# Alternating the pairs of an MLP's first product, using one raw weight buffer less per pair, and tying the row splits of its second product to its sums

## The chip, the cores and the metric

The kernel runs on one core of a Trainium2 chip. The metric is device time in microseconds (us) of one launch, median of three runs. In the profile PE is the matrix engine (TensorE), PEld its weight loads, DVE VectorE, ACT ScalarE, POOL GpSimd, and SP the engine that here only issues DMAs. "Lnnn" is a line of the kernel. A row such as "SPq" or "ACTq" is that engine's issuing side.

## The reference

One decoder layer for 1024 prompt tokens and 64 sample tokens (1088 in all), 1024 features. After a mixing part (an input projection, an RWKV-7 branch, a pooling branch, a merge), which the change does not touch, comes the channel mixer:

```
sh, sc, gt = ada_mod(c, lp["w_ada_mlp"], lp["b_ada_mlp"])
h = rms_norm(x, lp["norm_mlp"]) * (1 + sc) + sh
x = x + gt * (jnp.square(jax.nn.relu(h @ lp["w_ff1"])) @ lp["w_ff2"])
...
y = rms_norm(x, W["norm_final"])
```

`w_ff1` is 1024 x 4096 and `w_ff2` 4096 x 1024, all in fp32.

## The kernel before, in words

**A product.** Features lie on the 128 partitions, tokens along the free dimension. An fp32 matmul is made of three faster ones: each operand is split into a rounded part "hi" and a remainder "lo" (ACT copies hi, DVE or POOL subtracts to get lo), and hi·hi, hi·lo and lo·hi are added in PSUM. For weights `halves` does this (L186 to L195): a raw weight tile of 128 x 512 goes through ACT at L193 (`whi`) and DVE or POOL at L194 (`wlo`).

**The first MLP product (`ff1`, L1629)** works on 16 pairs `j`. A pair is two blocks of 128 hidden features; with the two halves of the input features and the two halves of the tokens (544 each) it is a 2 x 2 block product, done with seven block products `c` = 0 to 6 in place of eight, on sums and differences of the blocks. Each block product is 24 matmuls of 272 columns (`product`, L1466). `prep(c)` (L1491) loads raw weights (L1488), forms their sums and differences on DVE and POOL (L1502, L1504, L1505, L1515) and splits them; `run(c)` (L1524) issues the matmuls and takes the result out of PSUM, on ACT for c = 0, 1 (L1537, L1539, L1543) and on DVE for the others (L1555 to L1575), then squared ReLU on ACT (`relu2`, L1520). After c = 2 and c = 3 `combos` and the last lines of `run` form the sums that the second product needs and store them to DRAM (`d_ch`, `d_cl`; L1582 to L1609). Pairs 12 to 15 are "kept": they store their plain result (`d_hid`, L1570, L1578).

The first eight pairs (NE = 8) are "early": their products 0 and 1 run while the second token half is still being normalised, and the results go to DRAM (`d_u`, L1540, L1541) and come back later (L1499, L1500), when products 5, 6, 4, 2, 3 finish the pair. After these beginnings the order is: the eight early pairs with five products each, then pairs 8 to 15 with seven each (L1617 to L1619).

**Buffers.** Raw weights rotate through six tiles: two named `wraw` (every third) and four named `wr`. An early or full pair takes six: a, b, c, e, f are loaded, d = (b + c) - a is made in a tile of its own (L1503). Rows read back or built for later go through four tiles `hid`, larger ones through sixteen `hx`. Three PSUM tiles `pr` hold block products. Preparation runs four block products ahead of PE.

**The second MLP product (`ff2`, L1725)** takes groups of four pairs in the order 2, 0, 1 (GO). Each group has 28 block products in three phases: phase 0 with eight (c = 0, 1), phase 1 with twelve (6, 5, 2), phase 2 with eight (4, 3). Each ends with an addition into an accumulator on DVE (L1708), or for c < 4 of the first group with a copy on ACT (L1706). The moving rows for a coming phase are read from `d_ch` and `d_cl` by `spread` (L1642): ready-made pairs by two DMAs (L1649, L1650), others by one DMA into `hid` (L1654), an ACT copy (L1655) and a DVE subtraction (L1656), four rows at a time at set places in `ff2` (L1731 to L1744). After the last group eight plain products with the kept pairs follow (`hidden`, L1768), then the last part with the final norm.

**Order of work.** PE's instructions stand in the order in which the program is written (L1234), which a running estimate of PE time (`Pace`) arranges. The instructions of the other engines, and the DMAs on each issuing queue, are placed by a scheduler that plays the program through with its own estimates of times: an instruction stands in its engine's queue where its inputs are estimated to be ready, and the engine then works strictly through that queue. `ada` (L1341) loads modulation weights into `hid`; its last third waits until pair 7 is done (L1353).

Of the kernel before, what the change touches and what calls it, by code (L numbers as in the profile page):

```python
# [19 lines left out]
D = 1024  # L20
# [116 lines left out]
class K:  # L137
# [1187 lines left out]
    def phase2(self):  # L1325
# [15 lines left out]
        def ada():  # L1341
            yield lambda: ("or", 8) in self.done
            first = 4 * [behind]

            def tile():
                t = self.row(p, "hid", 4)[:, :1024]
                return first.pop()(t) if first else t

            for g in range(3):
                if g == 2:  # L1350

                    self.done.add("ada")
                    yield lambda: ("hid", NE - 1) in self.done  # L1353
                asb = p.tile([P, 512], F32, tag="wr2", bufs=4, name=self.nm("asb"))
                yield from self.ada_part("w_ada_mlp", g, tile, asb, self.aq, "b_mlp", (8 * g, 8 * g + 4), 5600, 2500, 19000 if g == 0 else 0)

# [43 lines left out]
        def norm2(i):  # L1400
# [42 lines left out]
            if i:  # L1443
                self.done.add(("C", 5))
                for c in (6, 4, 2, 3):
                    one = 1.0
                    if c in (4, 2):
                        j, h = (NE - 3, 1) if c == 4 else (NE - 1, 0)
                        yield lambda: ("early", j, h) in self.done
                        one = g2[:, c, 0:1]  # L1450
                        nc.scalar.activation(one, early[j]["S"]["o" if h else "u"][:, 0:1], AF.Copy)
                        nc.scalar.activation(one, self.kc("one0")[:, 0:1], AF.Copy)
# [24 lines left out]
        def pair_steps(j, early):  # L1477
# [5 lines left out]
            def raw(key, i, h):  # L1483
                self.nr += 1
                q, tag, bufs = (self.wp, "wraw", 2) if self.nr % 3 == 0 else (p, "wr2", 4)
                t = D[key] = q.tile([P, 512], F32, tag=tag, bufs=bufs, name=self.nm(tag))
                if i is not None:
                    nc.sync.dma_start(t, src(i, h))  # L1488
                return t

            def prep(c):  # L1491
                def go():
                    if c == 0:
                        return self.halves(raw("a", 0, 0), False)
                    if c == 5:
                        if early == 2:
                            raw("a", 0, 0)
                            S["u"], S["o"] = self.pair(p, "hid", 4, dt=F32)
                            nc.sync.dma_start(S["u"], self.d_u[0][j])  # L1499
                            nc.sync.dma_start(S["o"], self.d_u[1][j])  # L1500
                        b, cc = raw("b", 1, 0), raw("c", 1, 1)
                        nc.vector.tensor_tensor(cc, b, cc, op=ALU.add)  # L1502
                        d = raw("d", None, None)  # L1503
                        nc.vector.tensor_tensor(d, cc, D["a"], op=ALU.subtract)  # L1504
                        nc.gpsimd.tensor_tensor(b, D["a"], b, op=ALU.subtract)  # L1505
                        return self.halves(d, False)
                    if c == 1:
                        return self.halves(raw("e", 0, 1), False)
                    if c == 6:
                        return self.halves(D["b"], False)  # L1510
                    if c == 4:
                        return self.halves(D["c"], False)
                    if c == 2:
                        e = raw("e", 0, 1) if early == 2 else D["e"]
                        nc.gpsimd.tensor_tensor(e, e, D["d"], op=ALU.subtract)  # L1515
# [8 lines left out]
            def run(c):  # L1524
                def go(w):
                    if c in (0, 1):
# [10 lines left out]
                            nc.scalar.activation(v2(S["u"]), v, AF.Copy)  # L1537
                        elif early:
                            nc.scalar.activation(v2(S["o"]), v, AF.Copy)  # L1539
                            nc.scalar.dma_start(self.d_u[0][j], S["u"])  # L1540
                            nc.scalar.dma_start(self.d_u[1][j], S["o"])  # L1541
                        else:
                            nc.scalar.activation(v2(S["o"]), v, AF.Relu)  # L1543
                            nc.scalar.activation(S["o"], S["o"], AF.Square)
# [20 lines left out]
                    elif c == 2:  # L1565
# [1 line left out]
                        nc.vector.tensor_tensor(v2(o[:, HF:]), v2(S["u"]), v, op=ALU.add)  # L1567
                        relu2(o[:, HF:])
                        if kept:
                            nc.scalar.dma_start(self.d_hid[j - 4 * NG], o)  # L1570
                        else:
                            combos()
                    else:
# [1 line left out]
                        nc.vector.tensor_tensor(v2(o[:, :HF]), v2(S["u1"]), v, op=ALU.subtract)  # L1575
                        relu2(o[:, :HF])
                        if kept:
                            nc.scalar.dma_start(self.d_hid[4 + j - 4 * NG], o)  # L1578
                        else:
                            b21, b22, t2 = o[:, :HF], o[:, HF:], S["u1"]  # L1580
                            nc.vector.tensor_tensor(t2, b22, S["u"], op=ALU.subtract)
# [8 lines left out]
            def apart(c, x, hi):  # L1590

                if early:
                    nc.scalar.dma_start(self.d_ch[c][j], x)
                    return
                nc.scalar.activation(hi.bitcast(F32R), x, AF.Copy)
                nc.vector.tensor_tensor(x.bitcast(F32R), x, hi, op=ALU.subtract)
                nc.scalar.dma_start(self.d_ch[c][j], hi)
                nc.sync.dma_start(self.d_cl[c][j], x)

            def combos():  # L1600
# [13 lines left out]
        early, steps = [pair_steps(j, 1) for j in range(NE)], []  # L1614
        for j in range(0, NE, 2):
            steps += [early[j][0], early[j + 1][0], early[j][1], early[j + 1][1]]
        for j in range(16):  # L1617
            st = pair_steps(j, 2 if j < NE else 0)
            steps += [st[c] for c in ((5, 6, 4, 2, 3) if j < NE else (0, 5, 1, 6, 4, 2, 3))]  # L1619
        todo = list(steps)  # L1620
# [18 lines left out]

        E = {}  # L1640

        def spread(g, cs):  # L1642

            for c in cs:
                for k in range(4):
                    j = 4 * g + k
                    hi, lo = E[c, k] = self.pair(self.hx, "hx", 16) if c < 2 else self.pair(p, "t", 4) if c == 4 else MR()
                    if c < 3 and j >= NE:
                        nc.sync.dma_start(hi.bitcast(F32), self.d_ch[c][j])  # L1649
                        nc.sync.dma_start(lo.bitcast(F32), self.d_cl[c][j])  # L1650
                        continue
                    if k % 2 == 0:
                        two = self.pair(p, "hid", 4, dt=F32)
                    nc.sync.dma_start(two[k % 2], self.d_ch[c][j])  # L1654
                    nc.scalar.activation(hi, two[k % 2], AF.Copy)  # L1655
                    nc.vector.tensor_tensor(lo, two[k % 2], hi.bitcast(F32), op=ALU.subtract)  # L1656

        ACC = {}

        def sum_steps(g, mp):  # L1660
# [33 lines left out]
            def run(c):  # L1694
                def go(w):
# [8 lines left out]
                    acc, v = v2({1: a1, 2: a2, 3: a3}.get(c, a4)), ps[:, :, :HQ]  # L1704
                    if g == GO[0] and c < 4:
                        nc.scalar.activation(acc, v, AF.Copy)  # L1706
                    else:
# [17 lines left out]
        def ff2():  # L1725
            n = 0
            for i, (g, ph, (_, run, c)) in enumerate(sums):
                n = n + 1 if i and sums[i - 1][1] == ph else 0
                yield from run(made.pop(0))
                more()  # L1730
                if ph == 0 and n in (0, 2, 5) and (n or g != GO[0]):  # L1731
                    spread(g, ({0: 2, 2: 4, 5: 3}[n],))
                if ph == 1 and n in (2, 5):
                    if g in after:
                        spread(after[g], (n // 3,))
                    else:
                        for m in range(n // 3 * 4, n // 3 * 4 + 4):
                            self.xr[m] = HX(F32)
                            nc.sync.dma_start(self.xr[m], self.d_xr[m])
                if ph == 2 and n in (0, 4):  # L1740
                    if g in after:
                        spread(after[g], (6 - n // 4,))
                    else:
                        hidden(6, n // 2)  # L1744

        def whole():

# [17 lines left out]

        hid = {}

        def hidden(grp, part=None):  # L1768
            for j in range(4) if part is None else (part, part + 1):
                raw, hi, lo = self.row(p, "hid", 4), self.row(p, "mr", 16, F32R), self.row(p, "mr", 16, F32R)  # L1770
                nc.sync.dma_start(raw, self.d_hid[4 * (grp - 6) + j])
                nc.scalar.activation(hi, raw, AF.Copy)  # L1772
# [252 lines left out]
```

## Time and profile before

| what | us |
|---|---|
| median of three runs (1681.11 to 1681.25) | 1681.14 |
| the profiled execution's own time | 1678.41 |
| its span, first to last instruction | 1676.6 |
| PE busy in the span | 1606.3 |
| DVE busy | 1023.2 |
| ACT busy | 681.6 |
| POOL busy | 354.9 |
| mean granted TensorE clock | 0.986 |

The two products of the MLP lie between about 947 us (early beginnings) and 1567 us. In a list of waits a row reads: engine and line that waited, what released it, then microseconds in total, number of waits and the longest one. In a table by stage each engine has its busy time and, in brackets, its instructions; then come the granted clock (1.00 is full), the share of the 16 DMA engines and the rate in GB/s. In a timeline a row has its start, its duration, engine, line, operation, tiles, shapes and count, and in square brackets how long the engine had been idle and what released it.

### The profile page before, as it was taken

The page shows a single profiled execution, that of the slowest core. Times are in us where ns is not written, and L with a number is a line of the kernel's source. Part 1 is how long each engine was busy: PE and PEld are TensorE (multiplying, and loading weights), DVE is VectorE, ACT ScalarE, POOL GpSimd, SP SyncE. Part 2 cuts the span into 40 slices and gives each one's busy share as a digit, 9 for nine tenths or more (in the row PEclk, how much of TensorE's full clock was granted, in tenths as well). Part 3 has the DMA queues.
Part 4 walks back from the last instruction along what each step waited for, and adds up shares of the span by engine and source line. Part 5 has one row for each costly group of instructions (what it writes and reads, how often), then busy time and mean ns, then how long its engine had stood idle before and what let it go on. Part 6 is the DMA issues. An engine that isn't in the chain of part 4 may idle for free. (4 is left out here: it accounts for less than half of the span.)

```text
span 1676.6 us, 35210 instructions
## 1 busy us (share of the span) xinstructions
PE 1606.3 (96%) x14331; PEld 1496.1 (89%) x14331; DVE 1023.2 (61%) x1707; ACT 681.6 (41%) x1274; POOL 354.9 (21%) x392
## 2 busy tenths in 40 slices
PE   6999999998999999999999999999999899999997
PEld 3989878886888789879989999999999899999997
DVE  5676556845674556334546596765655387666766
ACT  4543333344334333422234475444555454333122
POOL 3311111000000000001722224542322041311221
PEclk9999999999998999999999999999999999999999
DMA  9333414232423242375984467656555875565112
GB/s 336 106 115 126 143 54 132 89 105 77 122 87 105 69 145 85 137 283 192 334 289 154 140 210 253 218 207 232 197 203 202 291 240 194 192 220 186 46 44 107
DMA packets 129473, 279.40 MB, mean 167 GB/s; under 512 B 16768, under 2 KB 31104, under 8 KB 129312
## 3 DMA queue, kind: packets, MB, share of 16 engines
q1 hardware_dynamic: 112992, 236.32, 40.9%
q10 hardware_dynamic: 14688, 35.17, 6.0%
q0 software_dynamic: 1632, 5.67, 1.0%
q8 instruction: 113, 1.85, 0.4%
q14 instruction: 48, 0.39, 0.1%
HBM read 198.15 MB, written 78.95 MB: 165 GB/s over the span
## 5 line engine op out<-in xcount | busy, mean ns | idle before, releaser
L170 PE MATMUL mm<-hx,whi 128*128 128x362 f32 (+1 forms) x1920 | 510.0, 347 | 6.4 <-ACT px L565 2.9
L170 PEld LDWEIGHTS mm<-hx,whi 128*128 128x128 f32 x1920 | 336.0, 191 | 42.7 <-issue 18.1
L170 PE MATMUL pr<-mr,whi 128*128 128x272 f32 x1792 | 340.1, 289 | 10.8 <-DVE hx L1575 6.8
L170 PE MATMUL mm<-hx,wlo 128*128 128x362 f32 (+1 forms) x960 | 317.0, 330 | 0.0
L170 PEld LDWEIGHTS pr<-mr,whi 128*128 128x128 f32 x1792 | 282.8, 190 | 14.5 <-issue 10.7
L170 PE MATMUL pr<-mr,wlo 128*128 128x272 f32 x896 | 259.0, 289 | 0.0
L193 ACT ACTIVATE whi<-wraw 128x512 fp32r<-128x512 f32 x201 | 126.3, 629 | 262.0 <-PE mm L170 80.8
L170 PEld LDWEIGHTS mm<-hx,wlo 128*128 128x128 f32 x960 | 183.9, 192 | 0.0
L194 DVE TENSOR_TENSOR wlo<-wraw,whi 128x512 fp32r<-128x512 f32 x146 | 107.4, 736 | 122.2 <-ACT whi L193 121.5
L170 PE MATMUL pr<-hx,whi 128*128 128x272 f32 x896 | 170.2, 289 | 7.5 <-ACT hx L1706 6.1
L170 PEld LDWEIGHTS pr<-mr,wlo 128*128 128x128 f32 x896 | 169.9, 190 | 0.0
L170 PE MATMUL mm<-mr,whi 128*128 128x272 f32 (+4 forms) x736 | 153.2, 302 | 0.4 <-DVE hx L1708 0.4
L170 PEld LDWEIGHTS pr<-hx,whi 128*128 128x128 f32 x896 | 141.4, 190 | 9.8 <-ACT hx L1706 6.4
L194 POOL TENSOR_TENSOR wlo<-wraw,whi 128x512 fp32r<-128x512 f32 x55 | 79.8, 1452 | 273.7 <-ACT whi L193 263.7
L193 ACT ACTIVATE whi<-wr 128x512 fp32r<-128x512 f32 x123 | 76.5, 627 | 136.9 <-PE pr L170 110.7
L170 PE MATMUL pr<-hx,wlo 128*128 128x272 f32 x448 | 129.4, 289 | 0.0
L170 PEld LDWEIGHTS mm<-mr,whi 128*128 128x128 f32 x736 | 119.1, 188 | 7.9 <-issue 5.0
L170 PE MATMUL mm<-mr,wlo 128*128 128x272 f32 (+4 forms) x368 | 110.1, 299 | 0.0
L194 DVE TENSOR_TENSOR wlo<-wr,whi 128x512 fp32r<-128x512 f32 x94 | 74.5, 793 | 25.3 <-ACT whi L193 25.2
L170 PEld LDWEIGHTS pr<-hx,wlo 128*128 128x128 f32 x448 | 84.9, 189 | 0.0
L170 PE MATMUL pr<-t,whi 128*128 128x272 f32 x448 | 84.4, 287 | 0.0
L1708 DVE TENSOR_TENSOR hx<-hx,pr 128x544 f32<-128x544 f32 x68 | 48.7, 716 | 46.9 <-PE pr L170 46.5
(386 smaller groups left out, 2641.3 us busy)
## 6 DMA issues: line engine op xcount, KB each, us to landing
wr<-in_w_ff SPq DMA_DIRECT2D x123, 256.0 KB, 3.2
wraw<-in_w_ff SPq DMA_DIRECT2D x85, 256.0 KB, 3.0
hid<-d_ch SPq DMA_DIRECT2D x72, 272.0 KB, 3.8
wraw<-in_w_in SPq DMA_DIRECT2D x68, 256.0 KB, 2.8
hid<-in_w_ada_mlp SPq DMA_DIRECT2D x24, 512.0 KB, 6.0
d_th<-px SPq DMA_DIRECT2D x22, 544.0 KB, 3.0
wt<-d_x SPq DMA_DIRECT2D x20, 544.0 KB, 4.2
d_ch<-hx SPq DMA_DIRECT2D x36, 272.0 KB, 3.9
```

The costliest lines, as they stand in the source:

```text
L170: return self.nc.tensor.matmul(out, lhsT, rhs, **kw)
L193: nc.scalar.activation(hi, raw, AF.Copy)
L194: (nc.gpsimd if pool else nc.vector).tensor_tensor(lo, raw, hi.bitcast(F32), op=ALU.subtract)
L1708: nc.vector.tensor_tensor(acc, acc, v, op=ALU.add)
```

## The change

- **Order:** an early pair's five products are followed by one full pair's seven: pairs 0, 8, 1, 9, ... 7, 15. The last third of `ada` now waits for pair 11 (NE + 3), which is then the eighth to finish.
- **Raw buffers:** tile d is gone. b becomes a - b on DVE (it was on POOL), and a becomes (b + c) - a in place. A pair takes five raw tiles.
- **Queues:** the stores that ACT issued in `ff1` (`d_u`, `d_ch`, `d_hid`) are issued by SP.
- **Row splits of the second product:** rows are read and split one or two per block product, and a split's ACT copy is tied to the block product's accumulator by `tie`: two one-column copies on ACT, the first reading the accumulator, the second setting the value 1.0 that the split takes as its scale. So a split can't stand in ACT's queue ahead of that sum.

```
-                    yield lambda: ("hid", NE - 1) in self.done
+                    yield lambda: ("hid", NE + 3) in self.done
...
                         b, cc = raw("b", 1, 0), raw("c", 1, 1)
+                        a = D["a"]
                         nc.vector.tensor_tensor(cc, b, cc, op=ALU.add)
-                        d = raw("d", None, None)
-                        nc.vector.tensor_tensor(d, cc, D["a"], op=ALU.subtract)
-                        nc.gpsimd.tensor_tensor(b, D["a"], b, op=ALU.subtract)
-                        return self.halves(d, False)
+                        nc.vector.tensor_tensor(b, a, b, op=ALU.subtract)
+                        nc.vector.tensor_tensor(a, cc, a, op=ALU.subtract)
+                        return self.halves(a, False)
...
-                        nc.gpsimd.tensor_tensor(e, e, D["d"], op=ALU.subtract)
+                        nc.gpsimd.tensor_tensor(e, e, D["a"], op=ALU.subtract)
...
-                            nc.scalar.dma_start(self.d_u[0][j], S["u"])
-                            nc.scalar.dma_start(self.d_u[1][j], S["o"])
+                            nc.sync.dma_start(self.d_u[0][j], S["u"])
+                            nc.sync.dma_start(self.d_u[1][j], S["o"])
...
-                            nc.scalar.dma_start(self.d_hid[j - 4 * NG], o)
+                            nc.sync.dma_start(self.d_hid[j - 4 * NG], o)
...
-                            nc.scalar.dma_start(self.d_hid[4 + j - 4 * NG], o)
+                            nc.sync.dma_start(self.d_hid[4 + j - 4 * NG], o)
...
-                    nc.scalar.dma_start(self.d_ch[c][j], x)
+                    nc.sync.dma_start(self.d_ch[c][j], x)
...
-                nc.scalar.dma_start(self.d_ch[c][j], hi)
+                nc.sync.dma_start(self.d_ch[c][j], hi)
...
-        for j in range(16):
+        for j in [j for k in range(NE) for j in (k, NE + k)]:
...
+        def one_row(g, c, k, one):
+            j = 4 * g + k
...
+            x = self.two[k % 2]
+            nc.sync.dma_start(x, self.d_ch[c][j])
+            nc.scalar.activation(hi, x, AF.Copy, scale=one)
+            nc.vector.tensor_tensor(lo, x, hi.bitcast(F32), op=ALU.subtract)
+
+        def tie(i, x):
+
+            one = g2[:, i % 8, 0:1]
+            nc.scalar.activation(one, x[:, 0:1], AF.Copy)
+            nc.scalar.activation(one, self.kc("one0")[:, 0:1], AF.Copy)
+            return one
...
-                if ph == 0 and n in (0, 2, 5) and (n or g != GO[0]):
-                    spread(g, ({0: 2, 2: 4, 5: 3}[n],))
-                if ph == 1 and n in (2, 5):
-                    if g in after:
-                        spread(after[g], (n // 3,))
...
-                if ph == 2 and n in (0, 4):
-                    if g in after:
-                        spread(after[g], (6 - n // 4,))
-                    else:
-                        hidden(6, n // 2)
+                one = lambda: tie(i, self.last)
+                rows = []
+                if ph == 0:
+                    rows = [(g, c, k) for c in ((2, 4, 3) if g != GO[0] else (4, 3)) for k in range(4)]
+                    rows = rows[2 * n:2 * n + 2]
+                elif g in after:
+                    rows = [(after[g], c, k) for c in ((0, 1) if ph == 1 else (6, 5)) for k in range(4)]
+                    rows = rows[n:n + 1] if ph == 2 else rows[n - 2:n - 1] if n > 1 else []
...
+                elif ph == 2 and n % 2 == 0:
+                    hidden(6, [n // 2], one())
+                if rows:
+                    apart_now = any(c > 2 or 4 * gr + k < NE for gr, c, k in rows)
+                    x = one() if apart_now else 1.0
+                    for r in rows:
+                        one_row(*r, x)
```

More of the change, by code (lines that the diff above doesn't have):

```diff
@@ L1449, in norm2 @@
                         yield lambda: ("early", j, h) in self.done
-                        one = g2[:, c, 0:1]
-                        nc.scalar.activation(one, early[j]["S"]["o" if h else "u"][:, 0:1], AF.Copy)
-                        nc.scalar.activation(one, self.kc("one0")[:, 0:1], AF.Copy)
+                        one = tie(c, early[j]["S"]["o" if h else "u"])
                     for k in range(4):
@@ L1486, in raw @@
                 t = D[key] = q.tile([P, 512], F32, tag=tag, bufs=bufs, name=self.nm(tag))
-                if i is not None:
-                    nc.sync.dma_start(t, src(i, h))
+                nc.sync.dma_start(t, src(i, h))
                 return t
@@ L1640, in phase2, with spread @@
         E = {}
-        def spread(g, cs):
+        def spread(g, cs, one=1.0):
             for c in cs:
                 for k in range(4):
[L1646 to L1656, printed above, removed]
+                    one_row(g, c, k, one)
+        def one_row(g, c, k, one):
+            j = 4 * g + k
+            hi, lo = E[c, k] = self.pair(self.hx, "hx", 16) if c < 2 else self.pair(p, "t", 4) if c == 4 else MR()
+            if c < 3 and j >= NE:
+                nc.sync.dma_start(hi.bitcast(F32), self.d_ch[c][j])
+                nc.sync.dma_start(lo.bitcast(F32), self.d_cl[c][j])
+                return
+            if k % 2 == 0:
+                self.two = self.pair(p, "hid", 4, dt=F32)
+            x = self.two[k % 2]
[7 more added lines that the diff above has]
+            return one
         ACC = {}
@@ L1703, in go @@
                     (a1, a4), (a2, a3) = ACC[mp]
-                    acc, v = v2({1: a1, 2: a2, 3: a3}.get(c, a4)), ps[:, :, :HQ]
+                    self.last = {1: a1, 2: a2, 3: a3}.get(c, a4)
+                    acc, v = v2(self.last), ps[:, :, :HQ]
                     if g == GO[0] and c < 4:
@@ L1730, in ff2 @@
                 more()
-                if ph == 0 and n in (0, 2, 5) and (n or g != GO[0]):
-                    spread(g, ({0: 2, 2: 4, 5: 3}[n],))
-                if ph == 1 and n in (2, 5):
-                    if g in after:
-                        spread(after[g], (n // 3,))
-                    else:
-                        for m in range(n // 3 * 4, n // 3 * 4 + 4):
-                            self.xr[m] = HX(F32)
-                            nc.sync.dma_start(self.xr[m], self.d_xr[m])
-                if ph == 2 and n in (0, 4):
-                    if g in after:
-                        spread(after[g], (6 - n // 4,))
-                    else:
-                        hidden(6, n // 2)
+                one = lambda: tie(i, self.last)
[6 more added lines that the diff above has]
+                    rows = rows[n:n + 1] if ph == 2 else rows[n - 2:n - 1] if n > 1 else []
+                elif ph == 1 and n in (2, 5):
+                    for m in range(n // 3 * 4, n // 3 * 4 + 4):
+                        self.xr[m] = HX(F32)
+                        nc.sync.dma_start(self.xr[m], self.d_xr[m])
+                elif ph == 2 and n % 2 == 0:
[5 more added lines that the diff above has]
+                        one_row(*r, x)
         def whole():
@@ L1766, in phase2, with hidden @@
         hid = {}
-        def hidden(grp, part=None):
-            for j in range(4) if part is None else (part, part + 1):
+        def hidden(grp, rows=range(4), one=1.0):
+            for j in rows:
                 raw, hi, lo = self.row(p, "hid", 4), self.row(p, "mr", 16, F32R), self.row(p, "mr", 16, F32R)
                 nc.sync.dma_start(raw, self.d_hid[4 * (grp - 6) + j])
-                nc.scalar.activation(hi, raw, AF.Copy)
+                nc.scalar.activation(hi, raw, AF.Copy, scale=one)
                 nc.vector.tensor_tensor(lo, raw, hi.bitcast(F32), op=ALU.subtract)
```

## The prediction, made before the result was known

> **What bounds the kernel now.** I read the page's head first, then PE's waits, then stages, then timelines round each stall.
>
> ```profile
> span 1676.6 us, 35210 instructions
> PE 1606.3 (96%) x14331; PEld 1496.1 (89%) x14331; DVE 1023.2 (61%) x1707; ACT 681.6 (41%) x1274; POOL 354.9 (21%) x392
> ```
>
> PE is the bound, and the change takes no matmul away. So it can only win back time in which PE waits or runs at a low clock, inside the MLP. By stage (early pairs; full pairs; passage to the second product; second product):
>
> ```profile
> 1012.00:1131.00 119.00, 110.69 (x856) 109.35 (x854) 85.12 (x103) 56.15 (x94) 57.85 (x35) 0.97 0.65 224
> 1131.00:1290.00 159.00, 159.00 (x1274) 155.06 (x1273) 91.40 (x127) 83.11 (x134) 47.37 (x34) 1.00 0.57 197
> 1290.00:1320.00 30.00, 23.86 (x182) 23.64 (x181) 12.72 (x18) 13.49 (x24) 2.00 (x2) 0.89 1.05 395
> 1320.00:1567.00 247.00, 244.05 (x1951) 243.09 (x1950) 169.67 (x226) 102.79 (x166) 60.06 (x42) 1.00 0.58 195
> ```
>
> Columns: stretch, length, PE, PEld, DVE, ACT, POOL, clock, DMA share, GB/s. Full pairs run without a gap; the other three stages have all the loss. PE's waits in the first, third and fourth stretch:
>
> ```profile
> PE pr L170 <- DVE hx L1575: 6.8, 5, 3.0
> PE pr L170 <- DVE hid L1555: 1.5, 2, 1.2
> ...
> PE pr L170 <- ACT hx L1706: 6.1, 1, 6.1
> ...
> PE pr L170 <- DVE hx L1708: 2.5, 2, 1.9
> PE mm L170 <- DVE hx L1708: 0.4, 1, 0.4
> ```
>
> That is 8.3 + 6.1 + 2.9 = 17.3 us, always for a PSUM tile not yet emptied. After the two long ones the clock is low (start, duration, count):
>
> ```profile
> 1069.58 0.79 PE L170 MATMUL pr<-mr,whi 128*128 128x272 f32 x2 [3.02 <-DVE hx L1575]
> ...
> 1075.80 0.41 PE L170 MATMUL pr<-mr,whi 128*128 128x272 f32 x2
> ...
> 1315.22 0.82 PE L170 MATMUL pr<-hx,whi 128*128 128x272 f32 x2 [6.14 <-ACT hx L1706]
> ...
> 1318.10 0.42 PE L170 MATMUL pr<-hx,whi 128*128 128x272 f32 x2
> ...
> 1161.14 127.04 PE pr L170 x1020
> ```
>
> The last row, of the chain of waits, gives the full rate: 127.04/1020 = 0.1245 us a matmul, 2.99 us for a block product of 24. From 1069.58 to 1075.80 there are 27 matmuls in 6.22 us where 3.36 would do, 2.9 lost; from 1315.22 to 1318.10 it is 13 in 2.88, 1.3 lost. The whole prize is therefore 17.3 + 2.9 + 1.3 = 21.5 us, 1.3%.
>
> **The change, part by part.**
>
> *Raw buffer and order (early pairs: 8.3 + 2.9 = 11.2 us).* What holds the emptying back is DVE's queue, which stands at L1502 for raw weights:
>
> ```profile
> DVE wr L1502 <- DMA wraw<-in_w_ff: 18.6, 5, 5.8
> ...
> SPq L1488 <- DVE wr L1504: 27.1, 7, 6.8
> SPq L1606 <- DVE hid L1605: 25.0, 8, 6.5
> SPq L1488 <- POOL wraw L1515: 22.4, 6, 5.6
> ```
>
> (The first row is of 1012 to 1131 us, the SP rows of 990 to 1140.) SP can't issue the next weights because tile d is still in use: L1515 is its last reader, L1504 one of a's. Behind the waiting L1502 stand the PSUM additions for which PE waits. Six tiles now serve six uses in 15 us of PE time; after the change five uses, every 15 and 21 us in turn, so demand falls from 6/15 = 0.40 to 10/36 = 0.28 a microsecond. DVE load falls as well: 85.12 of 119 us over early pairs, 91.40 of 159 over full ones; mixed, 176.5 of 278, 63%. L1505's subtraction joins DVE:
>
> ```profile
> L1502 DVE TENSOR_TENSOR wr<-wraw,wr x16: 684/693/1347, 988.0 to 1266.5; 128x512 f32<-128x512 f32 x16
> ...
> L1504 DVE TENSOR_TENSOR wr<-wr,wr x16: 691/1368/1789, 988.7 to 1267.3; 128x512 f32<-128x512 f32 x16
> ...
> L1505 POOL TENSOR_TENSOR wraw<-wr,wraw x16: 1293/1675/1798, 988.8 to 1267.4; 128x512 f32<-128x512 f32 x16
> ```
>
> On DVE it takes 0.69 us, like L1502. Its POOL form runs beside L1504 and stretches that from 0.69 to 1.37, so DVE gains 0.68 and pays 0.69: nothing. The Trainium skill, "SBUF — State Buffer", section "SBUF: two separate sides", has an exclusive port lock between these two engines, under which the loser blocks for the other's whole instruction. By that rule the stretch would be up to POOL's 1.68 and DVE would win 1.0 a pair; the median shows 0.68, so the trace bears out a conflict but not a whole block.
>
> What stays is ACT's halt at a squared ReLU of a re-read row, placed by the scheduler ahead of the landing:
>
> ```profile
> ACT hid L1521 <- DMA wr<-in_w_ff: 9.6, 2, 5.5
> ACT hid L1521 <- DMA hid<-d_u: 7.7, 2, 5.3
> ```
>
> That is 17.3 us in four halts, and now full pairs' c = 0 and 1 are emptied by ACT behind it. Weights are four block products (12 us) ahead, PSUM about two (6 us), so a 5.5 us halt just fits. I leave 2.5 us: the 1.5 at L1555 and one 1.0. Ends: 0 and the 11.2 of today. I take **-8.7**, as the full pairs' row shows no wait at all.
>
> *Stores to SP (passage: 6.1 + 1.3 = 7.4 us).*
>
> ```profile
> 1303.11 0.62 ACT L193 ACTIVATE whi<-wr 128x512 fp32r<-128x512 f32 x1
> 1310.68 0.33 ACTq L1570 DMA_DIRECT2D d_hid<-hx  x1
> 1311.06 0.66 ACT L1521 ACTIVATE hx<-hx 128x544 f32<-128x544 f32 x1 [7.33 <-DMA wr<-in_w_ff]
> ```
>
> ACT is free at 1303.7, but its next instruction is a store that is issued only when an earlier weight load has landed. L1521 and then L1706, which must empty PSUM, stand behind. The weights do not bind there: by the count of copies the two block products after the stall had their `whi` by the first of these rows. On SP the store holds no arithmetic. SP takes 60 issues more in the first product (16 of `d_u`, 36 of `d_ch`, 8 of `d_hid`), 0.33 each, 20 us of over 350. Their waits are the unknown: L1606 now waits 25.0/8 = 3.1 us a time with loads behind it; for the 60, between 0 and 60 x 3.1 = 186 us of a halted SP. I take near 0 at PE, because loads precede their use by the 12 us lead, and keep the other end for a rival. Pair 7 now stands in front of the burst, with seven stores of 272 KB more: 1.9 MB at 395 GB/s, 4.8 us of DMA time. There is a second thing left at this place. In the first group's phase 0 the emptying copies L1706 stand on ACT themselves, behind tied splits whose rows come late:
>
> ```profile
> 1309.21 3.19 SPq L1654 DMA_DIRECT2D hid<-d_ch  x4
> ...
> 1308.56 5.47 DMA wr<-in_w_ff
> ```
>
> Rows issued from 1309.2 that land after some 5.5 us are there at 1314.7 and later; without today's stall the third block product ends at 1312.2, so a split tied to it can hold ACT for 2.5 us. The next copy L1706 is due 3 us after that sum, so it is hardly late. I leave 1.5 us for both: **-5.9** (ends 0 and -7.4).
>
> *Ties (second product: 2.9 us).* Both waits for L1708 follow bursts of splits in DVE's queue:
>
> ```profile
> 1371.51 4.99 DVE L1656 TENSOR_TENSOR mr<-hid,mr 128x544 fp32r<-128x544 f32 x6
> 1376.42 0.71 DVE L1708 TENSOR_TENSOR hx<-hx,pr 128x544 f32<-128x544 f32 x1
> ...
> L1451 ACT ACTIVATE g<-hid x2: 192/198/203, 987.4 to 993.5; 128x1 f32<-128x1 f32 x2
> ...
> L1452 ACT ACTIVATE g<-kct x2: 188/195/202, 987.6 to 994.2; 128x1 f32<-128x1 f32 x2
> ...
> L1655 ACT ACTIVATE mr<-hid x44: 641/647/664, 1286.1 to 1481.9; 128x544 fp32r<-128x544 f32 x44
> ```
>
> One split a product ends such bursts in phases 1 and 2. The price is 52 ties of two small copies, 52 x 0.39 = 20 us of ACT, which is busy 102.79 of 247: covered. A tie waits for the addition; behind it in ACT's queue stand weight copies, 12 us ahead of need. Phase 0 is the tight place: addition 0.71, tie 0.39, two splits 1.30 on ACT, the last subtraction 0.72, then the next addition's turn: 3.1 us against 2.99. Over six products that is 0.8 us behind, within the PSUM lead; cover gone, 0.8 us in each of two groups. I leave 1.4: **-1.5** (ends -2.9 and +1.6). The later third of `ada` and the fewer copies of raw tiles cost nothing: the same loads and four 1 us groups of PE work at another place.
>
> **The sum:** -8.7 - 5.9 - 1.5 = -16.1 on the profiled execution's 1678.4, so 1662.3. The median shown is 2.7 above that execution; carried over, 1681.1 - 16.1 = **1665.0**. If all the loss went, 1681.1 - 21.5 = 1659.6; if only half of 21.5 did, 1670.4. That is the likeliest case's own range.
>
> **The rivals.**
>
> *The passage stays: its limit is the transfers.* For it: share 1.05 and 395 GB/s at 1290 to 1320; pair 7 adds 4.8 us in front. Against it: the weights needed were there. Time: 1681.1 - 8.7 - 1.5 = 1670.9 with the passage as it is, 1674 with 3 us more of it. The Trainium skill, "DMA: Bandwidth & Descriptors", section "Issuing engines are not separate DMA queues", says that all issuers share 16 engines and a second one saves only issue time; by that rule moving stores frees no bandwidth, and this rival follows. ACT's 7.33 us halt is what the rule leaves out.
>
> *It doesn't do what it says.* The early stalls hang on ACT's 17.3 us, not on tile d, and only the order of stalls changes: -3 to +1, 1678 to 1682. For it: ACT's halts are as long as DVE's 18.6. Against it: the stalls are in DVE's emptying.
>
> *Slower: SP's queue becomes the bound.* A store now waits in SP for ACT's squared ReLU, itself halted on a row that SP loads; the next pair's weights are behind the store. It decides once the waits of a pair's stores in a row pass 12 us of lead less 3.8 for a load and 2 for splitting, about 6 us; L1606 alone reaches 6.5. Then each early pair shows a stall like today's longest: 8 x 3.0 + two low clocks of 2.9 = 29.8 in place of 11.2, with the passage at worst unchanged: 1681.1 + 18.6 = 1699.7; with the passage won (-7.4), 1692.3; with a third of the pairs, about 1685.
>
> **How the numbers follow.** Forecast 45%; passage stays 23%; no effect 9%; slower 23%. A measurement can tell about 0.2% from no change, 3.4 us. Faster by more: 0.45 + 0.23 + a little of the third = 0.69; same 0.08; slower 0.23. The range runs from everything won, 1659.6, to the slower case at 1692.3; it leaves out about one in seven above and below.
>
> **What would show it.** Right: no PE wait over 2 us between 1012 and 1300 us, clock 1.00 there; L1502's wait for DMA well below 18.6; no ACT wait of 7 us at the passage and L1706's 6.1 gone; no row of six L1656 in a run. Wrong: SP waits over 6 us at the stores with PE waiting for `whi`; PE waits for L1537 or L1543 (ACT halted in full pairs); L1708's waits grown in phase 0.

## The result, and the profile after

The changed kernel takes as long as the one before: ratio 1.0009, 95% interval 0.9991 to 1.0028, medians 1684.05 and 1682.49 us of 14 runs each, side by side. Forecast were 16 us less. The profiled execution took 1679.0 us. The head of its page:

```profile
span 1677.3 us, 35282 instructions
PE 1608.4 (96%) x14331; PEld 1495.8 (89%) x14331; DVE 1024.6 (61%) x1723; ACT 710.8 (42%) x1378; POOL 322.0 (19%) x376
```

The table by stage, with the stretches of the prediction, and PE's waits in the first product and in the second:

```profile
1012.00:1131.00 119.00, 118.87 (x955) 118.56 (x953) 87.89 (x114) 63.71 (x105) 37.49 (x26) 1.00 0.61 207
1131.00:1290.00 159.00, 150.96 (x1165) 143.48 (x1165) 93.27 (x124) 72.91 (x118) 41.45 (x29) 0.97 0.58 200
1290.00:1320.00 30.00, 30.00 (x243) 29.98 (x242) 17.17 (x24) 19.06 (x37) 3.14 (x2) 1.00 0.99 352
1320.00:1567.00 247.00, 242.06 (x1931) 240.54 (x1930) 162.02 (x223) 127.50 (x262) 57.58 (x42) 1.00 0.63 209
```

```profile
PE wc L170 <- DMA hid<-in_w_ada_mlp: 7.3, 2, 6.5
PE pr L170 <- ACT hx L1534: 0.8, 1, 0.8
...
PE pr L170 <- DVE hx L1717: 2.7, 3, 1.1
PE pr L170 <- ACT whi L193: 1.2, 1, 1.2
PE pr L170 <- DVE wlo L194: 0.8, 1, 0.8
PE w L170 <- DVE hx L1717: 0.5, 1, 0.5
```

The first and third stretch, which had all of the large losses, are full: 118.87 of 119 us and 30.00 of 30. The second, which was full, now lacks 8 us, and PE there waits for something new: the modulation weights of `ada`. PE's timeline and SP's at that place:

```profile
1159.41 1.92 PE L170 MATMUL wc<-hid,sT 128*32 128x512 f32 x4 [6.52 <-DMA hid<-in_w_ada_mlp]
1162.09 1.92 PE L170 MATMUL wc<-hid,sT 128*32 128x512 f32 x4 [0.76 <-DMA hid<-in_w_ada_mlp]
1163.95 0.82 PE L170 MATMUL pr<-mr,whi 128*128 128x272 f32 x2
...
1167.20 0.28 PE L170 MATMUL pr<-mr,wlo 128*128 128x272 f32 x1
...
1171.15 1.07 PE L170 MATMUL wc<-hid,sT 128*32 128x512 f32 x8
...
1184.74 2.16 PE L170 MATMUL wc<-hid,sT 128*32 128x512 f32 x8
```

```profile
1153.23 0.32 SPq L1581 DMA_DIRECT2D d_ch<-hid  x1
1153.64 0.40 SPq L1594 DMA_DIRECT2D d_ch<-hid  x1
1154.10 0.44 SPq L290 DMA_DIRECT2D hid<-in_w_ada_mlp  x1
1154.63 1.02 SPq L1595 DMA_DIRECT2D d_cl<-hx  x2
1155.74 8.64 SPq L290 DMA_DIRECT2D hid<-in_w_ada_mlp  x4
```

The loads L290 come right behind the last stores that read pair 11's `hid` tiles: the first is issued at 1154.1 us, and PE had come to its matmul at 1152.9. In the kernel before, the first was issued at 1104.9 us for a matmul at 1136.1. PE idles 7.3 us, and what follows runs slowly: two groups of four take 1.92 us each where eight take 1.07 (2.8 lost), fourteen matmuls from 1163.95 to 1167.20 take 3.25 us where 1.74 would do (1.5), and the eight at 1184.74 take 1.1 more, as their weight loads (PEld) wait 1.0 us for `ada`'s last DMA. Together **12.7 us**. The granted clock reads 0.50 from 1159 to 1167 us. (The Trainium skill, "TensorE: Matmul & The Clock Gate", section "HAM oscillation — how this bites in real kernels", warns of idle gaps above about 3.4 us. The 6.5 us gap agrees; the 3.0 us gap in the kernel before, after which the clock was 0.50 as well, lies below that figure.)

**Stages.** One execution differs from the next before the MLP too: its first block product started between 943.3 and 953.2 us in the profiles here, although each engine works through the same order in the two kernels up to that place. So the MLP is measured by itself: the *first product* from the first 272-column matmul on `hx` to the last emptying for c = 3, the *second*, with the passage, from there to the last addition. The rows for before and after (first and last start are the two numbers ahead of the semicolon):

```profile
L170 PE MATMUL pr<-hx,whi x896: 282/287/596, 947.3 to 1504.9; 128*128 128x272 f32 x180
...
L1575 DVE TENSOR_TENSOR hx<-hx,pr x16: 706/709/722, 1016.9 to 1303.3; 128x544 f32<-128x544 f32 x16
...
L1708 DVE TENSOR_TENSOR hx<-hx,pr x68: 705/716/722, 1337.7 to 1565.3; 128x544 f32<-128x544 f32 x68
```

```profile
L170 PE MATMUL pr<-hx,whi x896: 282/287/396, 951.7 to 1505.6; 128*128 128x272 f32 x180
...
L1572 DVE TENSOR_TENSOR hx<-hx,pr x16: 704/714/716, 1017.5 to 1309.6; 128x544 f32<-128x544 f32 x16
...
L1717 DVE TENSOR_TENSOR hx<-hx,pr x68: 705/716/722, 1338.1 to 1566.5; 128x544 f32<-128x544 f32 x68
```

First product 356.0 to 357.9 us: -11.2 of old loss, +12.7 of new. Second 262.0 to 256.9: -7.4 at the passage, +2.3 elsewhere. Together that is 3.2 us less in this pair of executions; the ratio's interval, -1.5 to +4.7 us, does not reach that far, and with one profile of each kernel it stays open where the rest lies.

### The profile page after: what moved, and what is told of

Same layout as the page of the kernel before. It is cut to its first block, busy times and chain, and to the rows that moved or that the text cites. A ratio compares the mean times of both kernels' runs of the same rounds, so it can differ in the third digit from the quotient of the medians.

```text
span 1677.3 us, 35282 instructions
## 1 busy us (share of the span) xinstructions
PE 1608.4 (96%) x14331; PEld 1495.8 (89%) x14331; DVE 1024.6 (61%) x1723; ACT 710.8 (42%) x1378; POOL 322.0 (19%) x376
## 5 line engine op out<-in xcount | busy, mean ns | idle before, releaser
L193 ACT ACTIVATE whi<-wraw 128x512 fp32r<-128x512 f32 x192 | 120.6, 628 | 240.7 <-PE mm L170 82.8
L193 ACT ACTIVATE whi<-wr 128x512 fp32r<-128x512 f32 x132 | 82.7, 628 | 142.8 <-PE pr L170 117.6
L194 POOL TENSOR_TENSOR wlo<-wraw,whi 128x512 fp32r<-128x512 f32 x49 | 68.3, 1395 | 271.8 <-ACT whi L193 261.5
L194 POOL TENSOR_TENSOR wlo<-wr,whi 128x512 fp32r<-128x512 f32 x35 | 51.1, 1461 | 108.5 <-ACT whi L193 90.9
```

Source lines behind the costliest of these rows:

```text
L194: (nc.gpsimd if pool else nc.vector).tensor_tensor(lo, raw, hi.bitcast(F32), op=ALU.subtract)
```

## The experiments

All lengths are us of one profiled execution each; a ratio is to the kernel before, from runs on the same chip. "Waits" are PE's, first product from 1003 us on, second with the passage.

| run | first product | waits | second | waits | ratio, 95% interval |
|---|---|---|---|---|---|
| before | 356.0 | 8.3 | 262.0 | 9.0 | 1 |
| after | 357.9 | 8.1 | 256.9 | 5.2 | 1.0009, 0.9991 to 1.0028 |
| e1 after, ada after pair 12 | 348.8 | 4.3 | 261.4 | 5.8 | 0.9935, 0.9910 to 0.9959 |
| e2 after, ada's matmuls later | 353.5 | 5.8 | 261.1 | 7.1 | 0.9939, 0.9916 to 0.9962 |
| e3 before, stores on SP | 354.9 | 7.6 | 254.4 | 2.8 | 0.9941, 0.9915 to 0.9966 |
| e4 before, ties | 356.2 | 9.0 | 267.7 | 13.1 | 1.0028, 1.0010 to 1.0047 |
| e5 e1 without ties | 352.5 | 5.2 | 259.4 | 7.0 | 0.9924, 0.9898 to 0.9951 |
| e6 before, SP stores, no tile d | 354.5 | 7.7 | 259.1 | 5.8 | 0.9967, 0.9954 to 0.9981 |
| e7 before, no tile d | 352.4 | 6.3 | 267.9 | 12.5 | 0.9981, 0.9957 to 1.0004 |
| e8 before, new order | 364.5 | 14.8 | 266.2 | 10.8 | 1.0050, 1.0032 to 1.0068 |
| e9 e1, squared ReLU first | 343.5 | 0.0 | 260.4 | 6.0 | 0.9903, 0.9883 to 0.9922 |
| e10 e1, tile sequence as before | 348.6 | 4.2 | 261.5 | 7.0 | 0.9933, 0.9910 to 0.9955 |
| e11 before, tile sequence shifted | 357.9 | 9.5 | 266.0 | 12.0 | 1.0022, 1.0005 to 1.0040 |
| e12 e9 with e10 | 343.5 | 0.0 | 259.6 | 7.0 | 0.9907, 0.9885 to 0.9928 |
| e13 e12 without ties | 343.6 | 0.0 | 257.7 | 3.5 | 0.9878, 0.9854 to 0.9902 |
| e14 e9 without ties | 343.5 | 0.0 | 258.0 | 5.6 | 0.9892, 0.9863 to 0.9922 |
| e15 e13 with tile d | 346.9 | 1.5 | 256.4 | 2.6 | 0.9879, 0.9851 to 0.9908 |
| e16 before, squared ReLU first | 350.7 | 4.2 | 260.9 | 7.6 | 0.9980, 0.9964 to 0.9996 |
| e17 e13 in the old order, sequence shifted | 346.2 | 1.5 | 258.1 | 6.4 | 0.9922, 0.9901 to 0.9943 |

### Where the gain went: ada (e1, e2, e8)

e1, one constant of the changed kernel:

```
-                    yield lambda: ("hid", NE + 3) in self.done
+                    yield lambda: ("hid", NE + 4) in self.done
```

> The changed kernel with the last third of ada released one pair later (after pair 12, a kept pair that needs no hid tile, in place of pair 11). Theory 1 (the gain is given back at ada: its weights wait for hid tiles that pair 11 still holds): PE's 7.3 us wait for in_w_ada_mlp and the low clock behind it go, about 13 us in all, so 10 to 13 us below the changed kernel and about 9 to 12 below the kernel before (ratio 0.993 to 0.995). Theory 2 (hid tiles are short anywhere in the alternating order): the wait only moves, at least 5 us of it stays, ratio 0.998 to 1.003.

The wait for `in_w_ada_mlp` is gone and the first product is 9.1 us shorter; theory 1 holds. Pair 12 keeps nothing in `hid`, so the tiles are free: the first load is issued at 1155.0 us, for a matmul at 1187.3. But a wait of another kind stands there now:

```profile
PE pr L170 <- ACT hx L1534: 4.0, 3, 2.8
```

e2 leaves the release and puts PE's matmuls 12 us later in its order (`19000 if g == 0 else 12000 if g == 2 else 0`):

> The changed kernel with the release of ada's last third left after pair 11, but PE's first matmul of it put 12 us later in PE's order. Theory 1 (only the place of the matmuls in PE's order is too early for weights that land late): the first wait of 6.5 us goes, the others shrink below 1 us, ratio to before 0.993 to 0.995. Theory 2 (the hid tiles, now held 12 us longer, delay the rows of the next early pairs): a new wait of 3 us or more for DVE's emptying or for weights, ratio 0.998 or above.

The 6.5 us wait is gone, 1.4 us of waits for these weights are left, and the first product is 4.4 us shorter, less than half of e1's gain. Both mendings agree: the weights were late for their place in PE's fixed order.

e8 is the kernel before with only the order changed (`for j in [j for k in range(NE) for j in (k, NE + k)]`, and `NE + 3`):

> The kernel before with the alternating order alone (ada's last third after pair 11). Theory 1: the wait of PE for in_w_ada_mlp appears as in the changed kernel (5 us or more), the early pairs' waits fall to below 4 us, the passage keeps 6 us: ratio 0.999 to 1.004. Rival (the wait at ada needs the stores on SP, whose queue delays the release of hid tiles): no wait for in_w_ada_mlp above 2 us, ratio 0.994 to 0.998.

```profile
PE wc L170 <- DMA hid<-in_w_ada_mlp: 10.6, 3, 8.3
PE pr L170 <- ACT hx L1706: 6.1, 1, 6.1
PE pr L170 <- ACT hx L1537: 2.6, 3, 1.5
```

The order alone brings the wait for `ada`, larger still, so stores on SP are not its cause. Its ratio, 1.0050, is above theory 1's range. It also ends all waits for L1575, with tile d in use, and leaves 1.6 us for L1555.

### The stores (e3)

Six times `nc.scalar.dma_start` becomes `nc.sync.dma_start` in the kernel before.

> The kernel before with one part alone: the 60 stores of the first product issued by SP. Theory 1 (ACT's halt at a store made the stall at the passage): the 6.1 us wait for L1706 and the 1.3 us of low clock go, the early pairs' 8.3 us stay or change by 2 us; MLP stage 5 to 8 us shorter, ratio 0.995 to 0.998. Rival (transfers limit the passage): the wait stays at 4 us or more, ratio 0.999 to 1.001. Rival (SP's queue holds back weights): PE waits for whi appear, ratio above 1.002.

The passage has no wait left, and nothing comes instead: second product 254.4 us, 7.6 less, where 7.4 stood to be won. Both rivals fall: from 1290 to 1320 us the transfers ran at 387 GB/s, about the 395 of before, and PE was busy for all 30 us. The ratio, 0.9941, is a little below the range given. PE's waits from 1003 to 1330 us are only those of the early pairs:

```profile
PE pr L170 <- DVE hx L1575: 7.0, 4, 3.8
PE pr L170 <- DVE hid L1555: 0.6, 2, 0.3
```

### What held the early pairs (e6, e7, e15, e16, e17, e9)

e7 takes tile d away from the kernel before; e6 does it with the stores on SP. Both also shift the tiles of the second product's weights, which costs time there (next section), so their early pairs are compared and not their totals:

```
-                        d = raw("d", None, None)
-                        nc.vector.tensor_tensor(d, cc, D["a"], op=ALU.subtract)
-                        nc.gpsimd.tensor_tensor(b, D["a"], b, op=ALU.subtract)
-                        return self.halves(d, False)
+                        a = D["a"]
+                        nc.vector.tensor_tensor(b, a, b, op=ALU.subtract)
+                        nc.vector.tensor_tensor(a, cc, a, op=ALU.subtract)
+                        return self.halves(a, False)
...
-                        nc.gpsimd.tensor_tensor(e, e, D["d"], op=ALU.subtract)
+                        nc.gpsimd.tensor_tensor(e, e, D["a"], op=ALU.subtract)
```

> The kernel before with the raw tile d gone alone. Theory 1: waits in the early pairs fall from 8.3 to below 3 us, the passage keeps its 6.1 us, ratio 0.994 to 0.997. Rival (DVE's load): waits of 6 us or more, ratio 0.999 to 1.002.

> The kernel before with stores on SP and the raw tile d gone, in the old order of pairs. Theory 1 (the early pairs' 8.3 us of waits come from the raw tile): they fall below 3 us and the time is 5 to 9 us below that of stores alone, ratio 0.989 to 0.992. Rival (they come from DVE's load over eight early pairs in a row, which only the order spreads): waits of 6 us or more stay, ratio 0.993 to 0.995.

The waits stay at 6.3 us (8.3 before) and 7.7 us (7.6 in e3): theory 1, my reading of the profile, fails. DVE's waits in e7 from 1003 to 1131 us, then ACT's:

```profile
DVE wlo L194 <- ACT whi L193: 21.5, 7, 5.9
DVE wr L1502 <- DMA wr<-in_w_ff: 5.1, 2, 2.7
DVE wraw L1502 <- DMA wraw<-in_w_ff: 2.2, 1, 2.2
```

```profile
ACT hid L1521 <- DMA hid<-d_u: 20.3, 4, 6.9
...
ACT hid L1521 <- DMA wr<-in_w_ff: 7.6, 1, 7.6
```

The wait at L1502 did fall, from 18.6 to 7.3 us. In its place DVE waits 21.5 us for ACT's weight copies, against 12.6 in the kernel before,

```profile
DVE wlo L194 <- ACT whi L193: 12.6, 7, 4.1
```

and ACT halts 27.9 us at the squared ReLU of re-read rows, against 23.4 in the kernel before over the same stretch. ACT's weight copies stand behind these halts. e16 moves the squared ReLU, in the kernel before, to where the row is made, ahead of its store:

```
-                            nc.scalar.activation(v2(S["o"]), v, AF.Copy)
+                            nc.scalar.activation(v2(S["o"]), v, AF.Relu)
+                            nc.scalar.activation(S["o"], S["o"], AF.Square)
...
-                        if early:
-                            relu2(S["o"])
```

> The kernel before with one edit: the squared ReLU of the early pairs' first output block is done before it is stored. Theory 1 (without tile d, ACT's halts at re-read rows took over as what holds the early pairs; with tile d both hold them): early pairs' waits fall from 8.3 to 4 to 7 us only, since DVE still waits for raw weights; the passage keeps its 6 us; ratio 0.996 to 0.999. Rival (ACT's halts are the only cause): waits below 2 us, ratio 0.992 to 0.995.

> Stores on SP, tile d gone and the squared ReLU before the store, in the old order of pairs and without ties. Theory 1 (either the order or these two edits together end the early pairs' waits, because both DVE's wait for raw weights and its wait for ACT are then gone): waits in the early pairs below 2.5 us, first product 345 to 348 us, ratio 0.988 to 0.991. Rival (eight early pairs in a row load DVE too much whatever it waits for): waits of 5 us or more, ratio 0.993 to 0.996.

Alone it leaves 4.2 us. But it does not free ACT: ACT now stands 24.9 us at the store of the re-read row, which the kernel before issues on ACT too:

```profile
ACT hx L1521 <- DMA hid<-d_u: 24.9, 5, 6.7
```

With tile d gone too and stores on SP (e17) 1.5 us are left, in the old order. e17 differs from e6 by the squared ReLU alone, so without tile d and with stores on SP it is ACT's halt that makes the early pairs' waits: 7.7 us with it, 1.5 without. DVE's waits in e17 from 1003 to 1131 us:

```profile
DVE wr L1502 <- DMA wr<-in_w_ff: 18.3, 6, 4.2
DVE wraw L1502 <- DMA wraw<-in_w_ff: 6.5, 2, 3.9
DVE wlo L194 <- ACT whi L193: 3.3, 6, 0.7
```

DVE waits 24.8 us for raw weights there, longer than the 18.6 of the kernel before, and PE hardly notices; what fell is the wait for ACT, from 20.4 us in e6 to 3.3. So the sum of DVE's waits at L1502 was no measure of the damage. Whether tile d must go as well in the old order is not shown: no run has the squared ReLU first, stores on SP and tile d. e15 shows that in the new order tile d hardly matters:

> Stores on SP, alternating order with ada after pair 12, squared ReLU before the store, no ties, and the raw tile d kept (six raw tiles a pair; the sequence of tiles in the second product is then that of the kernel before by itself). Theory 1 (the order, not the raw tile, ends the early pairs' waits): no wait above 1.5 us in the first product and the same time within 0.1% as without tile d and with the same sequence. Rival (the raw tile matters in the alternating order): 3 us or more of waits for DVE's emptying, 3 to 8 us slower.

It has 1.5 us of waits, 1.0 of them for `ada`'s weights, and its time does not differ from e13's, though its first product is 3.3 us longer and its second 1.3 us shorter. DVE waits for raw weights from 1003 to 1290 us about as long as in e13 (21.9 us):

```profile
DVE wr L1502 <- DMA wraw<-in_w_ff: 22.4, 14, 3.4
```

In the new order, as in e17, such waits cost PE next to nothing. What the order does not mend is ACT's halt ahead of a full pair's first emptying, the 4.0 us of e1; e9 is e1 with the squared ReLU first:

> The changed kernel, ada after pair 12, and the squared ReLU of the early pairs' first output block done before it is stored, so that ACT no longer has a squared ReLU of a re-read row in its queue. Theory 1 (ACT's halts at such rows hold up the emptying of c = 0 in full pairs): PE's 4.0 us of waits for L1534 fall below 1 us, first product 4 to 6 us shorter, ratio to before 0.989 to 0.992. Rival (the waits come from ACT's load, or other halts): 3 us or more stay, ratio 0.992 to 0.995.

No wait from 1003 us to the end of the first product is left, and it takes 343.5 us.

### The second product (e4, e5, e10 to e14)

e4 is the kernel before with the reading of rows and the ties of the changed one:

> The kernel before with one part alone: rows of the second product read one or two at a time and tied to the sums. Theory 1 (ties end bursts of splits but make a loop of sum, tie, split and sum about as long as a block product): the 2.9 us of waits in the second product become 3 to 6, with waits for whi or wlo among them, ratio 1.000 to 1.002. Rival (the second product's new waits come from the alternating order or the shifted raw tiles): waits of 1.5 us or less, ratio 0.998 to 1.000.

The waits beyond the passage grow from 2.9 to 6.7 us, and the time by 0.28%; no wait for `whi` or `wlo` is among them. What DVE waits for in the second product of the changed kernel, and of the one before:

```profile
DVE mr L1657 <- ACT mr L1656: 17.4, 17, 2.6
...
DVE hx L1657 <- ACT hx L1656: 8.2, 11, 1.3
```

```profile
DVE mr L1656 <- ACT mr L1655: 2.3, 4, 1.2
```

A tied copy runs just ahead of its subtraction, so DVE stands 25.6 us at subtractions, with additions queued behind; before, most copies were done in time. That this is what delays the additions is argued from the rows, not shown by a run. Ties do not shorten the waits that they were made for.

e5 takes the ties out of e1:

> The changed kernel without the ties (rows read and split as before), with ada's last third after pair 12. Theory 1 (ties cost 2 to 3 us of waits in the second product, as the run with ties alone suggests): 2 to 5 us below the run with ties and the same ada place, ratio to before 0.990 to 0.993; the second product's waits fall from 5.8 to about 3 us. Rival (the ties' cost shows only together with the old order): ratio 0.993 to 0.996, like the run with ties.

Waits rise to 7.0 us, though the second product is 2.0 us shorter, and the time does not differ clearly from e1's. So something else had lengthened the second product: five raw tiles a pair in place of six shift which of its weights lie in `wraw` and which in `wr`. e11 does that alone to the kernel before, with `(self.nr + 2) % 3 == 0` in `sum_steps`; e10 undoes it in e1 with `+ 1`; e12 is e10 with e9's edit:

> The kernel before with only that sequence of raw tiles in the second product shifted as in the changed kernel. Theory 1: the second product's waits grow from 2.9 to 5 us or more, 2 to 5 us slower, ratio 1.001 to 1.003. Rival: waits of 3.5 us or less, ratio 0.999 to 1.001.

> The changed kernel, ada after pair 12, with the second product's raw weights taking the tiles wraw and wr in the sequence that they had in the kernel before (five raw tiles a pair had shifted it by one). Theory 1 (the shifted sequence makes the second product's longer waits): its waits fall from 5.8 to 3 us or less, second product 2 to 4 us shorter. Rival (the ties make them): 5 us or more stay, no change in time beyond 0.1%.

> The changed kernel with ada after pair 12, the squared ReLU before the store, and the sequence of raw tiles as before. Theory 1 (the three losses are separate): no PE wait above 1.5 us in the first product, 3 us or less in the second; 15 to 18 us below the kernel before, ratio 0.989 to 0.991. Rival (each mended wait is followed by the next): ratio 0.992 to 0.995, like the run with ada alone.

e11 is slower by 0.22%, waits up from 2.9 to 5.9 us. Undoing it beside the ties helps neither e10 nor e12. e13 and e14 complete the square without ties:

> Stores on SP, raw tile d gone, alternating order with ada after pair 12 and the squared ReLU before the store; no ties, and the second product's raw tiles in the sequence of the kernel before. Theory 1 (ties alone and the shifted sequence alone each lengthen the second product; without both it is as in the run with stores alone, 254 us): second product 253 to 256 us, waits 3 us or less, ratio to before 0.985 to 0.988. Rival (the second product's length depends on more than these two): 258 us or more, ratio 0.989 to 0.991.

> The same with the shifted sequence of raw tiles. Theory 1: waits for the additions of the second product of 5 us or more as in the other runs with shifted sequence and no ties, second product 257 to 260 us, 2 to 5 us slower than with the sequence of before. Rival: no difference between the two beyond 0.1%.

Second product with ties 260.4 (shifted) and 259.6, without 258.0 and 257.7. Each of the two costs something in the kernel before; in the mended kernel their ratios, 0.9878 to 0.9907, have intervals that overlap. That ties cost some 2 us there is likely, not shown. e13's 257.7 us lie between its two forecasts and 3.3 above e3's second product: what makes that difference is open. e13, with stores on SP, the new order, ada after pair 12, squared ReLU first, no tile d, no ties and the old sequence, is the best kernel run: **1661.42 us, ratio 0.9878 (0.9854 to 0.9902)**; e15 equals it.

## Why the prediction was wrong, point by point

- **The place of ada: the step that failed.** The prediction had: "The later third of `ada` and the fewer copies of raw tiles cost nothing: the same loads and four 1 us groups of PE work at another place." It cost 12.7 us and took back most of the gain. The loads are the same, but they need `hid` tiles. In the old place they followed an early pair, which takes one; now a full pair, which takes two for its last sums and stores. I counted the moved step's PE work and not the tiles that its DMAs wait for. "The fewer copies" failed as well: they shifted the second product's tiles (e11).
- **Early pairs, forecast -8.7.** All 11.2 us went, for another reason than the one given. "SP can't issue the next weights because tile d is still in use" stands in the rows, but taking tile d away changed PE's waits little (e7: 8.3 to 6.3; e3 to e6: 7.6 to 7.7). In the old order what had to go was ACT's halt (e6 to e17: 7.7 to 1.5, with DVE waiting at L1502 longer than before). In the changed kernel, which keeps that halt, the order is what ended the waits (e8).
- **ACT's halts, 2.5 us left.** Right in kind: full pairs' first emptying behind them. 0.8 us in the changed kernel, where the long wait probably hides the rest, 4.0 in e1.
- **Stores, forecast -5.9.** Right, and a little more: -7.4. e3 shows the mechanism alone. The Trainium skill's rule in "DMA: Bandwidth & Descriptors", section "Issuing engines are not separate DMA queues", that issuers share the engines, did not decide, as ACT's halt and not bandwidth made the stall: e3 ran the passage at 387 GB/s without a wait.
- **The subtraction on DVE, forecast nothing.** Right: DVE has 16 instructions more and 1.4 us more busy time. But the median of L1504 was misread as "a conflict but not a whole block": it mixes instructions that start before POOL's and after it. Where POOL's L1505 started first, L1504 ended 0.54 to 0.56 us after it, in all nine such cases of 16 (below, 1050.60 after 1050.05 and 1067.10 after 1066.55); in the other seven it took 0.69. So the rows do show DVE held until POOL's instruction was over.

```profile
1048.36 1.69 POOL L1505 TENSOR_TENSOR wraw<-wr,wraw 128x512 f32<-128x512 f32 x1 [7.10 <-DVE wr L1502]
1048.81 1.79 DVE L1504 TENSOR_TENSOR wr<-wr,wr 128x512 f32<-128x512 f32 x1
...
1064.94 1.61 POOL L1505 TENSOR_TENSOR wraw<-wr,wraw 128x512 f32<-128x512 f32 x1 [4.42 <-DVE wr L1502]
1065.45 1.65 DVE L1504 TENSOR_TENSOR wr<-wr,wr 128x512 f32<-128x512 f32 x1
```

- **Ties, forecast -1.5, ends -2.9 and +1.6.** Wrong in sign: +2.3 in the changed kernel, with the shifted tiles; alone (e4) waits are 3.8 us up. I priced the loop in phase 0, not DVE standing behind each copy.
- **Slower by SP's queue.** It did not come: e3 has no new wait.

The forecast's 1665.0 is about what the kernel takes once `ada` and ACT's halts are mended (e9: 1664.8). That is luck in part: e9 has an edit that the forecast did not have, its first product is 12.5 us shorter than before where 8.7 was forecast, and its second 1.6 shorter where 7.4 was forecast.

## What to carry to other kernels

A step that is moved takes its buffers along: before moving it, list for each of its DMAs the tile that it lands in, who holds that tile at the new place, and when the last store out of it has landed. Where an engine waits in turn for two things, taking one away may only show the other, so look up what the next instruction in its queue would wait for. Don't issue a store that may have to wait on an engine that empties PSUM (e3), and don't place that engine's work on a row before the row can be there (e6 against e17).

## What the runs showed that I had not expected

The low clock after a gap can outlast it, and its cost depends on when it sets in. In the traces the granted clock is 0.50 from 1068.9 to 1075.7 us and from 1311.3 to 1318.1 us in the kernel before, 6.8 us both times. The first stretch set in near the end of a 3.0 us gap, so 6.2 us of work ran slowly; the second began inside a 6.1 us gap, and only 2.9 us did. In the changed kernel it lasts 10.2 us, from 1156.8 to 1167.1. Gaps of like length differ: in e6 one of 2.91 us before 1054.9 brought no low clock, one of 2.95 us before 1073.5 brought 3.4 us. Which of the rotating tiles a weight takes, with the same number of tiles, was worth 0.22% (0.05 to 0.40%) in e11. The profiled executions differ by up to 9.9 us in when the MLP begins, so a stage is better compared by its own length than by the total of one execution.
